# y of eight heads in one burst, the gate's samples in pairs, and three other moves in a one-layer hybrid decoder step

## The chip, the cores and the metric

The kernel runs on one core of a Trainium2 chip. The metric is the device time of one execution in microseconds. It computes in float32 throughout; its large matrix products run as three products of split operands (below). The engines are named as in the profile: PE (TensorE) with its weight loads PEld, DVE (VectorE), ACT (ScalarE), POOL (GpSimd) and SP, which issues most DMAs.

## The reference

One layer with two parts, for 256 rows of a prompt and 8 × 8 sample rows (320 columns together):

```
h    = rms_norm(x) ; proj = h @ w_in           # 2048 -> gate u, gate v, z, x|B|C, dt
gate_out = gelu(u) * (tril(W_s) @ layer_norm(gelu(v)) + b_s)     # 16 heads of 128, chunks of 128 rows
xBC  = silu(causal_conv4(xBC)) ; dt = softplus(dt + bias)
y    = (C B^T * exp(segment sums of dt*a)) @ (x*dt)              # inside a chunk, per head
     + exp(da) * C @ state                                       # from the state before the chunk
ssm_out = rms_norm_by_group((y + d*x) * silu(z))                 # 32 heads of 64 in 4 groups
state' = decay * state + B^T (decay * x * dt)
x1   = x + rms_norm([gate_out | ssm_out] @ w_out)
out  = x1 + rms_norm( (gelu(g) * u) @ w_down ),  g, u = causal_conv3(rms_norm(x1) @ w_up)
```

The gate's sample rows use the first 8 × 8 corner of W_s of each head. Outputs are the rows, the last states, the last rows of both convolutions and LayerNorm's rows of the last chunk (chunk_v).

## The kernel before

All activations stand transposed, features on the 128 partitions and the 320 rows of prompt and samples in the columns. A weight comes from HBM in slabs of 128 × 1024. ACT rounds a slab (`whi`, L128), DVE takes the remainder (`wlo`, L130), each with three buffers. For each 128 × 128 block PE runs three matmuls of 320 columns, whi·h_hi (L141), whi·h_lo (L142) and wlo·h_hi (L143). `project` does this for the columns of w_in and w_up into four large PSUM buffers (`ps`), `chunk_out` for w_out by 512 of its rows (`pd`), whose result DVE adds up in `acc`.

The work between these streams is written as generators. `project` and `chunk_out` call `tick()` at set places, which runs the next piece of the first generator up to its next `yield`. From that order of emission and from priorities, the framework that builds the program decides each engine's order by its own model of when things are ready; on the chip each engine takes its instructions strictly in that order. `tc.issue_after(x)` asks that an instruction be placed behind x.

Small results share four PSUM buffers (`misc`, tag ms): transposes, the gate's `sg`, y (`y_ps`), the sums of squares and the last states (`fin_ps`).

The pieces that the change touches:

- `layer_norm` (L651): after v of the gate is made and turned, its rows `vt` (64 of samples in the third block) are normalised in quarters of 512 columns. A quarter needs a row of the gains `lg` and one of the biases `lb` on all partitions. Each has two buffers, loaded by POOL's DMA queue. The third and fourth quarters' loads (L669) are emitted behind the steps that free a buffer.
- `gate_mix` (L689), once for each group of four heads: two matmuls of 128 columns for the prompt's chunks (L710), one of 64 columns for the samples (L711) with `wS`, the masked corner spread to 64 × 64 and zero in the lower 64 partitions. All are plain fp32.
- `ssd` (L769), once for each of four groups of eight heads, 128 × 128 pieces of fp32. `decays` makes for one head the matrix of decays times C·B from the running sums `cs` (loaded from DRAM for each pair of heads): DVE subtracts and clips in three pieces (L889), ACT takes the exponential (L891), DVE multiplies (L893). For each pair ACT also makes `cpx` (L882) and POOL multiplies it by C. `products` (L896) then runs y of a pair: eight matmuls in column halves of PE, each of which is two in the trace, and a DVE addition (L914). Today four heads' decays are followed by two pairs' products, then the other four.
- the convolution's `silu` on ACT (L426 and L427), which needs another table of ACT than the exponential.
- the stage of x1 (`x1_ready`, L1031): behind the last `pd`, DVE scales and adds x (L1036, L1037), ACT rounds (L370, `h_hi`), DVE takes the remainder (L371, `h_lo`), and the first product with w_up can start. Beside it `renewals` (L1147) adds the last states of groups 1 to 3 on POOL (L1158) and stores them by ACT's DMA queue (L1159).

Of the kernel before, what the change touches and what calls it, by code (L numbers as in the profile page):

```python
# [9 lines left out]
F32 = mybir.dt.float32  # L10
# [7 lines left out]
P = 128  # L18
NP = 256
# [15 lines left out]
def hybrid_step(  # L35
# [357 lines left out]
    with ExitStack() as mctx:  # L393
# [3 lines left out]
        pts = op.tile([P, 24, 3], F32, name="pts")  # L397
        LP = 347

        def conv_proj(c0, k0, out, soon=0):  # L400

            def evac(j, ps):
                with tc.high_priority(offset=soon) if soon else nullcontext():
                    conv(j, ps)

            def conv(j, ps):
                k = k0 + j
                pad = spare_pads.pop(0) if spare_pads and j % 2 else op.tile([P, LP], F32, tag="pad", name="pad", bufs=3)
                tokp = pad[:, 259:347].rearrange("p (b r) -> p b r", r=11)
                with first():  # L410
                    pool.memset(pad[:, 0:3], 0.0)
                    pool.tensor_copy(tokp[:, :, 0:3], sst[:, k])
# [12 lines left out]
                o = out(j)  # L425
                act.activation(o[:, :NP], t[:, :NP], AF.Silu)  # L426
                act.activation(o[:, NP:NT].rearrange("p (b t) -> p b t", b=NB),  # L427
                               t[:, 259:347].rearrange("p (b r) -> p b r", r=11)[:, :, 0:TS], AF.Silu)
            project(w_in, c0, evac, quiet=4)

        def heads_in(g):
# [117 lines left out]
        with tc.tile_pool(name="gp", bufs=1) as gp:  # L549
# [14 lines left out]
            for q in (2, 3):  # L564
                dve.tensor_tensor(out=heads4, in0=heads4, in1=ident[:, NH * q:NH * q + NH], op=ALU.add)

            wS = gp.tile([P, 4, NB, TS], F32, name="wS")
            pool.memset(wS[NS:], 0.0)

            x_asked = []  # L570
            x_sq = []
# [19 lines left out]
                            dve.tensor_tensor(out=acc[:, 0:2, :], in0=acc[:, 0:2, :], in1=acc[:, kt:kt + 2, :], op=ALU.add)  # L591

            def turned(g, vf):
                if g == 0:
                    pool.memset(vt[NS:, 2], 0.0)
                for c, (o, n) in enumerate(TOK):
                    ps = misc("vt_ps")
                    for j in range(4):
                        pe.transpose(ps[:n, P * j:P * j + P], vf[:, j, o:o + n], ident)  # L599
                    act.copy(vt[:n, c, 512 * g:512 * g + 512], ps[:n])  # L600
# [50 lines left out]
            def layer_norm():  # L651

                mv = gp.tile([P, 3, 2], F32, name="mv")
                pool.memset(mv, 1.0)
                for c, (o, n) in enumerate(TOK):
                    st = gp.tile([P, 4, 6], F32, tag="bn", name="bn", bufs=2)
                    for q in range(4):
                        dve.bn_stats(st[:n, q, :], vt[:n, c, 512 * q:512 * q + 512])
                    dve.bn_aggr(mv[:n, c, :], st[:n].rearrange("p a b -> p (a b)"))
                    yield  # L660
                lr = rsqrt_of(mv[:, :, 1], 1.0, 3)
                rows = []

                def load(q):
                    cs = slice(512 * q, 512 * q + 512)
                    for name, src in (("lg", gate_ln_g), ("lb", gate_ln_b)):
                        rows.append(gp.tile([P, 512], F32, tag=name, name=name, bufs=2))
                        with tc.issue_after(after_v[0]):
                            pool.dma_start(rows[-1], src[0:1, cs].broadcast_to([P, 512]))  # L669
                load(0)  # L670
                load(1)
                yield
                for q in range(4):
                    for c, (o, n) in enumerate(TOK):
                        v = vt[:n, c, 512 * q:512 * q + 512]
                        dve.scalar_tensor_tensor(out=v, in0=v, scalar=mv[:n, c, 0:1], in1=rows[2 * q][:n], op0=ALU.subtract, op1=ALU.mult)
                        dve.scalar_tensor_tensor(out=v, in0=v, scalar=lr[:n, c:c + 1], in1=rows[2 * q + 1][:n], op0=ALU.mult, op1=ALU.add)
# [10 lines left out]

            def gate_mix(g, uf, res):  # L689
                wT = gp.tile([P, 4, P], F32, tag="wT", name="wT", bufs=1)  # L690
                w8 = gp.tile([NS, 4, TS], F32, tag="w8", name="w8", bufs=1)
# [6 lines left out]
                with tc.issue_after(rsqrt_ins[1]):  # L698
                    dve.tensor_tensor(out=wT, in0=wT, in1=upper.unsqueeze(1).to_broadcast([P, 4, P]), op=ALU.mult)
                    for j in range(4):  # L700
                        dve.tensor_tensor(out=wS[:NS, j], in0=w8[:, j].unsqueeze(1).to_broadcast([NS, NB, TS]),
                                          in1=upper_s[:NS].rearrange("p (b t) -> p b t", b=NB), op=ALU.mult)
                yield
                hi, lo = out_parts(hp, "o")
                res += hi, lo
                for j in range(4):
                    fs = slice(512 * g + P * j, 512 * g + P * j + P)
                    ps = misc("sg")
                    for c in range(2):
                        pe.matmul(ps[:, P * c:P * c + P], vt[:, c, fs], wT[:, j, :], start=True, stop=True)  # L710
                    pe.matmul(ps[:, NP:NT], vt[:, 2, fs], wS[:, j].rearrange("p b t -> p (b t)"), start=True, stop=True)  # L711
# [32 lines left out]
        with tc.tile_pool(name="sd", bufs=1) as sd:  # L744
# [23 lines left out]

            def ssd(g):  # L769

                xs = x_of[g]
                h0 = 8 * g
                bs = slice(P * g, P * g + P)

# [6 lines left out]

                def load_sums(j):

                    cs = sd.tile([P, 2, NT], F32, tag="cs", name="cs", bufs=3)
# [50 lines left out]
                pe.matmul(ps, btok[:, 0, bs], x0d, start=True, stop=True)  # L835
# [40 lines left out]
                def decays(hl):  # L876
                    j, i = hl // 2, hl % 2
                    at = places(hl)
                    if i == 0:
                        cs = sums_of.pop(j)  # L880
                        cpx = sd.tile([P, 2, P], F32, tag="cpx", name="cpx", bufs=2)
                        act.activation(cpx, cs[:, :, at[1][0]:at[1][0] + P], AF.Exp)  # L882
# [31 lines left out]
                    dve.scalar_tensor_tensor(out=y, in0=y, scalar=d_col[:, 4 * g + j:4 * g + j + 1], in1=ps[:, :NT],  # L914
                                             op0=ALU.mult, op1=ALU.add)
# [12 lines left out]

# [126 lines left out]
    with tc.tile_pool(name="fp", bufs=1) as fp:  # L1055
# [91 lines left out]
        def renewals():  # L1147
# [7 lines left out]
            for g, s1, x1d, _ in rest:  # L1155
                yield
                yield
                pool.tensor_tensor(out=s1, in0=s1, in1=x1d, op=ALU.add)  # L1158
                act.dma_start(o_ssm_p[g], s1)  # L1159

            def load(g, i):

# [148 lines left out]
def laid_out(a):  # L1311
# [7 lines left out]
    def states(v, n):  # L1319
# [20 lines left out]
        "gate_w8": np.concatenate([w8] * NB),  # L1340
# [43 lines left out]
```

## Time and profile before

| | us |
|---|---|
| median of three runs | 1774.44 (1773.45 to 1777.11) |
| profiled execution | 1774.31 |
| its span | 1772.6 |
| mean granted TensorE clock | 0.999 |

The profile's page gives the busy time of each engine in the span, the chain of work that ended last (followed back from the last instruction through what released each step), and groups of instructions. The trace beneath it gives single instructions by time. A row of the timeline has the start, the length, the engine, the line, the operation with output and inputs, the tile of PE that it uses, shapes, how many are taken together, and in brackets the idle time before it with what ended it. On PE the length of a matmul is longer than its step to the next one, since they overlap. What a matmul costs is the difference of two starts.

### The profile page before, as it was taken

What the parts mean: (1) busy time and instruction counts of PE and PEld (TensorE: products, weight loads), DVE (VectorE), ACT (ScalarE), POOL (GpSimd) and SP (SyncE); (2) the same over time, 40 slices, a digit from 0 to 9 for tenths busy, and PEclk for the clock granted to TensorE, in tenths of its full rate; (3) what the DMA queues carried; (4) which work ended last, traced back from release to release, by engine and by line L of the source; (5) the groups of instructions that cost most, each with busy time, mean ns of one, the idle gap of its engine ahead of it and who ended that gap; (6) DMA issues with size and microseconds to landing.
All of it is one profiled execution on the core that took longest, in us unless ns stands there. A gap on an engine that the chain in (4) does not pass through costs nothing.

```text
span 1772.6 us, 31221 instructions
## 1 busy us (share of the span) xinstructions
PE 1765.2 (100%) x12223; PEld 1740.8 (98%) x12223; DVE 1183.2 (67%) x2052; ACT 800.8 (45%) x1111; POOL 281.5 (16%) x593
## 2 busy tenths in 40 slices
PE   9999999999999999999999999999999999999998
PEld 9999999999999999998999999999999999999998
DVE  7448854657877777678866666666666565656475
ACT  7344545333545454445645434343434343433335
POOL 2003210000111111012322212021101010101004
PEclk9999999999999999999999999999999999999999
DMA  7455554445664644444555656566554444444443
GB/s 251 138 167 167 191 156 149 155 152 183 226 208 150 206 154 151 154 164 155 169 190 191 210 177 201 188 196 200 185 187 153 148 155 147 157 148 152 153 148 107
DMA packets 228562, 303.04 MB, mean 171 GB/s; under 512 B 19488, under 2 KB 150656, under 8 KB 228224
## 3 DMA queue, kind: packets, MB, share of 16 engines
q1 hardware_dynamic: 216560, 281.27, 49.6%
q10 hardware_dynamic: 10448, 15.57, 2.4%
q0 software_dynamic: 1408, 4.23, 0.8%
q8 instruction: 96, 1.57, 0.4%
q14 instruction: 50, 0.41, 0.1%
HBM read 283.44 MB, written 17.58 MB: 170 GB/s over the span
## 4 chain that ended last, share of the span: by engine, by line
PE 98%; DVE 1%; DMA 0%; issue 0%; SPq 0%; POOL 0%; ACT 0%; DVEq 0%; ACTq 0%
PE ps L141 21%; PE ps L143 21%; PE ps L142 21%; PE pd L141 10%; PE pd L142 10%; PE pd L143 10%; PE y_ps L904 1%; PE sg L710 0%; PE yo_ps L853 0%; PE up_ps L1198 0%; PE tsum L282 0%; PE xt_ps L382 0%; PE vt_ps L599 0%; DMA vf<-in_w_in 0%; PE s_ps L835 0%; PE x1p L1233 0%
## 5 line engine op out<-in xcount | busy, mean ns | idle before, releaser
L130 DVE TENSOR_TENSOR wlo<-wraw,whi 128x1024 fp32r<-128x1024 f32 x470 | 581.4, 1237 | 383.2 <-ACT whi L128 380.6
L128 ACT CAST whi<-wraw 128x1024 fp32r<-128x1024 f32 x470 | 492.2, 1048 | 703.0 <-PE ps L142 411.5
L141 PE MATMUL ps<-h_hi,whi 128*128 128x320 f32 x2528 | 782.7, 310 | 0.0
L142 PE MATMUL ps<-h_lo,whi 128*128 128x320 f32 x2528 | 780.2, 309 | 1.4 <-DVE h_lo L371 1.4
L143 PE MATMUL ps<-h_hi,wlo 128*128 128x320 f32 x2528 | 779.7, 309 | 0.2 <-DVE wlo L130 0.2
L142 PEld LDWEIGHTS ps<-h_lo,whi 128*128 128x128 f32 x2528 | 475.0, 188 | 2.8 <-DVE h_lo L371 1.9
L141 PEld LDWEIGHTS ps<-h_hi,whi 128*128 128x128 f32 x2528 | 474.7, 188 | 3.1 <-issue 1.6
L143 PEld LDWEIGHTS ps<-h_hi,wlo 128*128 128x128 f32 x2528 | 474.6, 188 | 0.9 <-DVE wlo L130 0.7
L141 PE MATMUL pd<-fhi,whi 128*128 128x320 f32 x704 | 217.3, 309 | 0.0
L143 PE MATMUL pd<-fhi,wlo 128*128 128x320 f32 x704 | 217.3, 309 | 0.0
L142 PE MATMUL pd<-flo,whi 128*128 128x320 f32 x704 | 217.3, 309 | 0.0
L141 PE MATMUL pd<-ohi,whi 128*128 128x320 f32 x448 | 138.7, 310 | 0.0
L142 PE MATMUL pd<-olo,whi 128*128 128x320 f32 x448 | 138.6, 310 | 0.0
L143 PE MATMUL pd<-ohi,wlo 128*128 128x320 f32 x448 | 138.3, 309 | 0.0
L142 PEld LDWEIGHTS pd<-flo,whi 128*128 128x128 f32 x704 | 132.1, 188 | 0.7
L143 PEld LDWEIGHTS pd<-fhi,wlo 128*128 128x128 f32 x704 | 132.1, 188 | 0.0
L141 PEld LDWEIGHTS pd<-fhi,whi 128*128 128x128 f32 x704 | 132.1, 188 | 0.0
L234 DVE TENSOR_TENSOR acc_ffn<-acc_ffn,pd 128x320 f32<-128x320 f32 x160 | 77.3, 483 | 33.2 <-PE pd L143 32.0
L1091 POOL COPY ptf<-pad 128x2 f32<-128x2 f32 x88 | 22.6, 258 | 405.6 <-DVE pad L1079 405.0
L141 PEld LDWEIGHTS pd<-ohi,whi 128*128 128x128 f32 x448 | 84.1, 188 | 0.9 <-issue 0.4
L142 PEld LDWEIGHTS pd<-olo,whi 128*128 128x128 f32 x448 | 84.1, 188 | 0.7 <-issue 0.4
L143 PEld LDWEIGHTS pd<-ohi,wlo 128*128 128x128 f32 x448 | 84.1, 188 | 0.2 <-issue 0.2
(303 smaller groups left out, 1582.6 us busy)
## 6 DMA issues: line engine op xcount, KB each, us to landing
wraw<-in_ffn_w_up SPq DMA_DIRECT2D x176, 512.0 KB, 3.5
wraw<-in_w_in SPq DMA_DIRECT2D x142, 512.0 KB, 3.5
wraw<-in_ffn_w_down SPq DMA_DIRECT2D x88, 512.0 KB, 3.3
wraw<-in_w_out SPq DMA_DIRECT2D x64, 512.0 KB, 3.3
st<-in_state_ssm SPq DMA_DIRECT2D x64, 256.0 KB, 4.6
out_ssm_state_sample<-st ACTq DMA_DIRECT2D x32, 256.0 KB, 2.6
cs<-dacs_d SPq DMA_DIRECT2D x16, 320.0 KB, 4.5
xr<-in_xT SPq DMA_DIRECT2D x4, 640.0 KB, 4.6
```

Of the source, the lines that this page charges most:

```text
L128: act.copy(hi[:, :m], raw[:, :m])
L130: dve.tensor_tensor(out=lo[:, :m], in0=raw[:, :m], in1=hi[:, :m].bitcast(F32), op=ALU.subtract)
L141: pe.matmul(ps, whi, xhi, start=first, stop=False)
L142: pe.matmul(ps, whi, xlo, start=False, stop=False)
L143: newest[0] = pe.matmul(ps, wlo, xhi, start=False, stop=last).ins
L234: dve.tensor_tensor(out=acc[:, nb, :], in0=acc[:, nb, :], in1=ps[:, :NT], op=ALU.add)
L904: pe.matmul(ps[64 * i:64 * i + 64, cols], w(hl), x(hl, m, cpx), tile_position=(0, 64 * i), **flags)
L1091: pool.tensor_copy(ptf[:, k, :], pad[:, 256:258])
```

## The change

1. `ssd`: all eight heads' decays come first, then four pairs' products in one go. `cs` and `cpx` get four buffers, and all four loads of cs are asked for together.
2. `gate_mix`: the sample rows of an odd head are copied by DMA (POOL's queue, behind LayerNorm's quarters) into the lower 64 partitions of the even head's columns, and `wS` becomes block diagonal for two heads, so that one matmul of 128 columns serves both. The odd head has none.
3. `renewals`: additions and stores of the last states are put under `issue_after(whole[KD - 1])`, the last split of x1.
4. `layer_norm`: all eight row loads are emitted ahead of the quarters; those of the last two go into two buffers of the tag vf.
5. `ssd`: the exponential of cpx comes under `issue_after(last_silu)`.

The scratch for DMAs that POOL issues goes from 4096 to 1024.

```diff
+                made = act.activation(o[:, NP:NT]..., AF.Silu)
+                silus.append(made.ins)
...
-            wS = gp.tile([P, 4, NB, TS], F32, name="wS")
-            pool.memset(wS[NS:], 0.0)
+            wS = gp.tile([P, 2, 2, NB, TS], F32, name="wS")
+            pool.memset(wS, 0.0)
...
-                if g == 0:
-                    pool.memset(vt[NS:, 2], 0.0)
...
-                load(0)
-                load(1)
+                both = [("lg", gate_ln_g), ("lb", gate_ln_b)]
+                for q in range(2):
+                    rows.append([load(q, src, gp.tile([P, 512], F32, tag=name, name=name, bufs=2)) for name, src in both])
+                late = [gp.tile([P, 4, NT], F32, tag="vf", name=name, bufs=2).rearrange("p k n -> p (k n)") for name, _ in both]
+                for q in range(2):
+                    rows.append([load(2 + q, src, row[:, 512 * q:512 * q + 512]) for row, (_, src) in zip(late, both)])
...
-                        if c == 2 and q < 2:
-                            load(q + 2)
+                        if c == 2:
+                            two = vt[:, 2, 512 * q:512 * q + 512].rearrange("p (i r f) -> p i r f", r=2, f=P)
+                            pool.dma_start(two[NS:, :, 0], two[:NS, :, 1])
...
-                    pe.matmul(ps[:, NP:NT], vt[:, 2, fs], wS[:, j].rearrange("p b t -> p (b t)"), start=True, stop=True)
+                    if j % 2 == 0:
+                        pe.matmul(ps[:, NP:NP + 2 * NS], vt[:, 2, fs], wS[:, j // 2].rearrange("p r b t -> p (r b t)"), start=True, stop=True)
+                        of_two = ps[:, NP:NP + 2 * NS].rearrange("p (r b t) -> p r b t", r=2, b=NB)
...
-                                      in0=ps[:, NP:NT].rearrange("p (b t) -> p b t", b=NB),
+                                      in0=of_two[:, j % 2],
...
-                xs = x_of[g]
+                xs, last_silu = x_of[g], silus[-1]
...
-                sums_of = {j: load_sums(j) for j in range(3)}
+                sums_of = {j: load_sums(j) for j in range(4)}
...
-                        act.activation(cpx, cs[:, :, at[1][0]:at[1][0] + P], AF.Exp)
+                        with tc.issue_after(last_silu):
+                            act.activation(cpx, cs[:, :, at[1][0]:at[1][0] + P], AF.Exp)
...
-                for j in range(0, 4, 2):
-                    for hl in range(2 * j, 2 * j + 4):
-                        decays(hl)
-                        yield
+                for hl in range(8):
+                    decays(hl)
                     yield
+                yield
+                for j in range(4):
                     products(j)
-                    products(j + 1)
-                    if j == 0:
-                        sums_of[3] = load_sums(3)
...
-                pool.tensor_tensor(out=s1, in0=s1, in1=x1d, op=ALU.add)
-                act.dma_start(o_ssm_p[g], s1)
+                with tc.issue_after(whole[KD - 1]):
+                    pool.tensor_tensor(out=s1, in0=s1, in1=x1d, op=ALU.add)
+                    act.dma_start(o_ssm_p[g], s1)
...
-    nc = _bacc.Bacc("TRN2", target_bir_lowering=False, num_devices=1, dynamic_dma_scratch_size=4096)
+    nc = _bacc.Bacc("TRN2", target_bir_lowering=False, num_devices=1, dynamic_dma_scratch_size=1024)
```

What this makes of the engines' orders is shown at three places. First PE at group 1's last y, before (y_ps is y of a pair of heads, xt_ps the transposes of the next group's x, pd the product with w_out):

```order
L141 MATMUL pd_11_6327<-ohi,whi 128x320
L904 MATMUL y_ps<-cs,xdt 64x128
L382 MATMUL xt_ps<-ident,xs 128x128 x2
L904 MATMUL y_ps<-cs,xdt 64x128 x3
L904 MATMUL y_ps<-cpx,s_5500 64x128 x2
L904 MATMUL y_ps<-cs,xdt 64x64 x2
L382 MATMUL xt_ps<-ident,xs 128x128 x6
```

and now, at the only y of group 1 (the rows between are three more pairs of the same form):

```order
L143 MATMUL pd_5_6123<-ohi,wlo 128x320
L912 MATMUL y_ps<-cs,xdt 64x128 x4
L912 MATMUL y_ps<-cpx,s_5465 64x128 x2
L912 MATMUL y_ps<-cs,xdt 64x64 x2
...
L142 MATMUL pd_6_6208<-olo,whi 128x320
L382 MATMUL xt_ps<-ident,xs 128x128 x3
L143 MATMUL pd_6_6208<-ohi,wlo 128x320
```

Y of group 1 was spread over six pieces with 95, 21 and fewer stream matmuls between; now all 32 matmuls stand together, 120 stream matmuls behind yo, with five of them before the first transposes. In groups 0 and 2 two bursts 72 matmuls apart become one at 120 behind yo, in group 3 (59 and 72) one at 118.

Second PE at one group of the gate, before and now (sg is the gate's sum of a head, vt LayerNorm's rows):

```order
L710 MATMUL sg<-wT,vt 128x128 x2
L711 MATMUL sg<-wS,vt 128x64
```

```order
L715 MATMUL sg<-wT,vt 128x128 x2
L717 MATMUL sg<-wS,vt 128x128
L715 MATMUL sg<-wT,vt 128x128 x4
L717 MATMUL sg<-wS,vt 128x128
L715 MATMUL sg<-wT,vt 128x128 x2
```

The first piece stood four times in a group, once for each head: twelve matmuls. Now there are ten, and the sample matmul has 128 columns.

Third POOL and ACT in the stage of x1. POOL with its waits, before and now (sq is a sum of squares, s a group's state, pad the up-projection's rows):

```order
L300 TENSOR_TENSOR sq_8507<-sq_8507,sq 128x320 [waits Activation_49,Pool_49] x11
L1158 TENSOR_TENSOR s_5500<-s_5500,x1d 128x512 [waits Activation_49]
L1076 MEMSET pad 128x2 [waits DMAHW3_49,DMAHW4_49,DMAHW2_49,DMAHW5_49,DMAHW1_49,DMAHW6_49,DMAHW0_49,DMAHW7_49,DVE_49,PE_49]
```

```order
L300 TENSOR_TENSOR sq_8500<-sq_8500,sq 128x320 [waits Activation_49,Pool_49] x11
L1164 TENSOR_TENSOR s_5465<-s_5465,x1d 128x512 [waits Activation_49]
L1081 MEMSET pad 128x2 [waits DMAHW3_49,DMAHW4_49,DMAHW2_49,DMAHW5_49,DMAHW1_49,DMAHW6_49,DMAHW0_49,DMAHW7_49,DVE_49,PE_49]
```

The addition stands three times in a row in both, at the same place, and waits for the same engine at the same count. ACT there, before and now (h_hi the rounded x1, x1d the copy of fin_ps):

```order
L1014 COPY x1d<-fin_ps 128x512
L1159 DMA out_ssm_state_prompt<-s_5500 128x512
L370 ACTIVATE h_hi<-acc_mix,prm 128x320
L1041 COPY x1d<-fin_ps 128x512
L370 ACTIVATE h_hi<-acc_mix,prm 128x320
```

```order
L370 ACTIVATE h_hi<-acc_mix,prm 128x320 x4
L1165 DMA out_ssm_state_prompt<-s_5465 128x512
L128 CAST whi<-wraw 128x1024
L1165 DMA out_ssm_state_prompt<-s_6378 128x512
L1165 DMA out_ssm_state_prompt<-s_7382 128x512
L128 CAST whi<-wraw 128x1024
```

On ACT the three stores moved from among the first copies to behind the last ones.

More of the change, by code (lines that the diff above doesn't have):

```diff
@@ L398, in hybrid_step @@
         LP = 347
+        silus = []
         def conv_proj(c0, k0, out, soon=0):
@@ L426, in conv @@
                 act.activation(o[:, :NP], t[:, :NP], AF.Silu)
-                act.activation(o[:, NP:NT].rearrange("p (b t) -> p b t", b=NB),
-                               t[:, 259:347].rearrange("p (b r) -> p b r", r=11)[:, :, 0:TS], AF.Silu)
+                made = act.activation(o[:, NP:NT].rearrange("p (b t) -> p b t", b=NB),
+                                      t[:, 259:347].rearrange("p (b r) -> p b r", r=11)[:, :, 0:TS], AF.Silu)
+                silus.append(made.ins)
             project(w_in, c0, evac, quiet=4)
@@ L662, in layer_norm, with load @@
                 rows = []
[L664 to L669, printed above, removed]
-                load(0)
-                load(1)
+                def load(q, src, row):
+                    with tc.issue_after(after_v[0]):
+                        pool.dma_start(row, src[0:1, 512 * q:512 * q + 512].broadcast_to([P, 512]))
+                    return row
+                both = [("lg", gate_ln_g), ("lb", gate_ln_b)]
[4 more added lines that the diff above has]
+                    rows.append([load(2 + q, src, row[:, 512 * q:512 * q + 512]) for row, (_, src) in zip(late, both)])
                 yield
@@ L675, in layer_norm @@
                         v = vt[:n, c, 512 * q:512 * q + 512]
-                        dve.scalar_tensor_tensor(out=v, in0=v, scalar=mv[:n, c, 0:1], in1=rows[2 * q][:n], op0=ALU.subtract, op1=ALU.mult)
-                        dve.scalar_tensor_tensor(out=v, in0=v, scalar=lr[:n, c:c + 1], in1=rows[2 * q + 1][:n], op0=ALU.mult, op1=ALU.add)
-                        if c == 2 and q < 2:
-                            load(q + 2)
+                        dve.scalar_tensor_tensor(out=v, in0=v, scalar=mv[:n, c, 0:1], in1=rows[q][0][:n], op0=ALU.subtract, op1=ALU.mult)
+                        dve.scalar_tensor_tensor(out=v, in0=v, scalar=lr[:n, c:c + 1], in1=rows[q][1][:n], op0=ALU.mult, op1=ALU.add)
+                        if c == 2:
+                            two = vt[:, 2, 512 * q:512 * q + 512].rearrange("p (i r f) -> p i r f", r=2, f=P)
+                            pool.dma_start(two[NS:, :, 0], two[:NS, :, 1])
                         yield
@@ L700, in gate_mix @@
                     for j in range(4):
-                        dve.tensor_tensor(out=wS[:NS, j], in0=w8[:, j].unsqueeze(1).to_broadcast([NS, NB, TS]),
-                                          in1=upper_s[:NS].rearrange("p (b t) -> p b t", b=NB), op=ALU.mult)
+                        rs = slice(NS * (j % 2), NS * (j % 2) + NS)
+                        dve.tensor_tensor(out=wS[rs, j // 2, j % 2], in0=w8[rs, j].unsqueeze(1).to_broadcast([NS, NB, TS]),
+                                          in1=upper_s[rs].rearrange("p (b t) -> p b t", b=NB), op=ALU.mult)
                 yield
@@ L782, in load_sums @@
                 def load_sums(j):
-                    cs = sd.tile([P, 2, NT], F32, tag="cs", name="cs", bufs=3)
+                    cs = sd.tile([P, 2, NT], F32, tag="cs", name="cs", bufs=4)
                     o = NS * (j // 2)
@@ L880, in decays @@
                         cs = sums_of.pop(j)
-                        cpx = sd.tile([P, 2, P], F32, tag="cpx", name="cpx", bufs=2)
-                        act.activation(cpx, cs[:, :, at[1][0]:at[1][0] + P], AF.Exp)
+                        cpx = sd.tile([P, 2, P], F32, tag="cpx", name="cpx", bufs=4)
+                        with tc.issue_after(last_silu):
+                            act.activation(cpx, cs[:, :, at[1][0]:at[1][0] + P], AF.Exp)
                         pool.tensor_tensor(out=cpx, in0=cpx, in1=cT[:, g, P:2 * P].unsqueeze(1).to_broadcast([P, 2, P]),
@@ L1339, in laid_out @@
         "gate_wT": w_s.transpose(2, 0, 1),
-        "gate_w8": np.concatenate([w8] * NB),
+        "gate_w8": np.concatenate([w8] * (P // TS)),
         "gate_b_s": a["gate_b_s"], "ssm_dt_bias": a["ssm_dt_bias"], "ssm_a_log": a["ssm_a_log"],
```

2 lines of the change are left out of this document (1 added, 1 removed).

## The prediction

> **What bounds the kernel now.** I read the page first, then the chain of waits, then what PE waits for, then the timelines of the five places that the change touches.
>
> ```profile
> PE 1765.2 (100%) x12223; PEld 1740.8 (98%) x12223; DVE 1183.2 (67%) x2052; ACT 800.8 (45%) x1111; POOL 281.5 (16%) x593
> PE 98%; DVE 1%; DMA 0%; issue 0%; SPq 0%; POOL 0%; ACT 0%; DVEq 0%; ACTq 0%
> L128 ACT CAST whi<-wraw 128x1024 fp32r<-128x1024 f32 x470 | 492.2, 1048 | 703.0 <-PE ps L142 411.5
> PE ps L142 <- DVE h_lo L371: 1.4, 2, 1.2
> PE s_ps L835 <- POOL xde L821: 0.2, 1, 0.2
> ```
>
> PE is busy for 1765.2 of 1772.6 us and carries 98% of the chain. The work that feeds it has room: ACT's weight split L128 stood idle 411.5 us because it waited for PE. So time can only come from fewer or shorter PE instructions, from fewer joints between different kinds of them, or from the few places where something holds PE up. Of those the list of PE's waits (the last two rows, from that view) has one over a microsecond, 1.4 us on h_lo in the x1 stage. A microsecond off DVE, ACT or POOL is worth nothing elsewhere. The step of the steady stream, from the timeline:
>
> ```profile
> 181.79 0.31 PE L143 MATMUL ps<-h_hi,wlo 128*128 128x320 f32 x1
> ...
> 187.07 0.31 PE L143 MATMUL ps<-h_hi,wlo 128*128 128x320 f32 x1
> ```
>
> 36 matmuls in 5.28 us: 0.147 us each, start to start (the 0.31 is latency).
>
> **y of eight heads in one burst.** PE's timeline at group 0's first y of four heads:
>
> ```profile
> 477.94 0.31 PE L143 MATMUL pd<-ohi,wlo 128*128 128x320 f32 x1
> 478.18 0.66 PE L904 MATMUL y_ps<-cs,xdt 128*64 128x128 f32 x8
> 478.67 0.39 PE L904 MATMUL y_ps<-cpx,s 128*64 128x128 f32 x4
> 478.89 0.72 PE L904 MATMUL y_ps<-cs,xdt 128*64 128x64 f32 x12
> 479.44 0.39 PE L904 MATMUL y_ps<-cpx,s 128*64 128x128 f32 x4
> 479.66 0.28 PE L904 MATMUL y_ps<-cs,xdt 128*64 128x64 f32 x4
> 479.87 0.42 PE L141 MATMUL pd<-ohi,whi 128*128 128x320 f32 x1
> 480.13 0.31 PE L142 MATMUL pd<-olo,whi 128*128 128x320 f32 x1
> ```
>
> Two heads repeat after 479.44 − 478.67 = 0.77 us. The burst lasts 479.87 − 478.18 = 1.69, which is 2 × 0.77 and 0.15 for its start. The change of kind costs more at both ends: 478.18 − 477.94 = 0.24 before it and 480.13 − 479.87 = 0.26 after it, against 0.147, so 0.09 and 0.11. A burst thus has a fixed price of 0.15 + 0.20 = 0.35 us. The matmuls themselves stay the same in number and shape. In groups 0, 2 and 3 two bursts become one (the chain lists 1.69 twice in each): 3 × 0.35 = **1.05 us**. Group 1 is scattered now, and the chain shows six pieces:
>
> ```profile
> 490.70 1.69 PE y_ps L904 x32
> ...
> 559.27 0.36 PE y_ps L904 x2
> ...
> 560.41 1.69 PE y_ps L904 x27
> ...
> 576.22 0.36 PE y_ps L904 x2
> ...
> 577.08 0.91 PE y_ps L904 x13
> ...
> 581.27 0.36 PE y_ps L904 x2
> ...
> 582.00 0.92 PE y_ps L904 x13
> ```
>
> They sum to 4.60 us; one burst of eight heads takes 0.15 + 4 × 0.77 = 3.23: 1.37 less. Five pairs of joints go as well, at most 5 × 0.20 = 1.0; the last two pieces stand beside transposes, whose own joints with the stream remain or even get one more place, so I take 0.75. Group 1 gives **2.1 us** (1.4 to 2.4).
>
> **Gate's samples in pairs.** One head of the gate on PE's timeline:
>
> ```profile
> 259.97 0.66 PE L710 MATMUL sg<-wT,vt 128*128 128x128 f32 x4
> 260.47 0.33 PE L711 MATMUL sg<-wS,vt 128*128 128x64 f32 x2
> 260.64 0.66 PE L710 MATMUL sg<-wT,vt 128*128 128x128 f32 x4
> ```
>
> A head takes 260.64 − 259.97 = 0.67 us for six passes (each fp32 matmul runs as two), 0.112 a pass, although two of the six move 64 columns and the others 128. So the step is not set by the columns, and a sample pass of 128 columns should cost the same 0.112. Now two heads share one sample matmul: 24 passes of a group become 20. 4 × 0.112 = 0.45 in each of four groups: **1.8 us**. Bounds: nothing more than this, and 1.4 if the wide passes bring back 0.02 each at the joints. The price is paid outside PE: four copies of 64 rows of vt by POOL's DMA queue behind LayerNorm. Each cost POOL about the 0.54 of a load's issue in the row at 172.01 below and a landing of some 4 us, and nobody reads them before 259.36, over 70 us later. wS's clearing on POOL and its products on DVE are as many as before. Nothing on PE.
>
> **LayerNorm's rows early.** POOL's and DVE's timelines, two pieces of the chain on PE:
>
> ```profile
> 172.01 0.54 POOL L669 DMA_DIRECT2D lb<-in_gate_ln_b  x1 [0.40 <-DVE vt L677]
> ...
> 175.53 0.75 DVE L677 SCALAR_TENSOR_TENSOR vt<-vt,rs_r,lb 128x512 f32<-128x512 f32 x1 [3.81 <-DMA lb<-in_gate_ln_b]
> ...
> 181.29 0.37 PE ps L143
> ...
> 187.38 0.27 PE ps L141
> ```
>
> The third and fourth quarter's lb is issued only when DVE has freed a row, and DVE then stands 3.81 us before it. Its weight splits fall behind, and 6 and 12 us later two of PE's steps last 0.37 and 0.27 in place of 0.147: 0.22 + 0.12 = **0.35 us**. Now all eight loads go ahead of the LayerNorm in POOL's order, the late ones into buffers of vf that are free some 35 us earlier, so DVE does not stand. If the two steps had another cause, 0.
>
> **Last states' additions.** The timeline of the x1 stage (POOL, DVE, PE):
>
> ```profile
> 814.35 1.26 POOL L1158 TENSOR_TENSOR s<-s,x1d 128x512 f32<-128x512 f32 x1 [7.11 <-ACT x1d L1014]
> ...
> 814.91 1.05 DVE L1037 TENSOR_TENSOR acc_mix<-acc_mix,xr 128x320 f32<-128x320 f32 x1
> ...
> 816.80 0.48 DVE L1037 TENSOR_TENSOR acc_mix<-acc_mix,xr 128x320 f32<-128x320 f32 x1
> ...
> 817.14 2.76 POOL L1158 TENSOR_TENSOR s<-s,x1d 128x512 f32<-128x512 f32 x2 [1.53 <-ACT x1d L1041]
> 817.20 1.55 DVE L371 SCALAR_TENSOR_TENSOR h_lo<-acc_mix,prm,h_hi 128x320 fp32r<-128x320 f32 x1
> ...
> 818.81 0.41 PE L142 MATMUL ps<-h_lo,whi 128*128 128x320 f32 x1 [1.17 <-DVE h_lo L371]
> ...
> 820.30 0.41 PE L142 MATMUL ps<-h_lo,whi 128*128 128x320 f32 x1 [0.20 <-DVE h_lo L371]
> ```
>
> DVE's addition of xr takes 1.05 us beside POOL's first addition and 0.48 when POOL is quiet, and the 1.55 of h_lo falls under POOL's other two. This is what holds PE for 1.17 and 0.20. Freed of it PE would win 1.4 from the waits and up to 0.57 (1.05 − 0.48) at the head of the stage, 1.9 together. But I count **nothing**. The new wait names the last h_hi copy, an ACT instruction, and the order of instructions shows what it reaches: ACT's three output DMAs move behind the last x1 copies, while POOL's three additions keep their place and wait for ACT's copy of fin_ps as before. The ACT issues that move wait for nothing that PE needs. Bounds: −1.9 if the additions do move, and +0.3 if the moved issues delay a weight split.
>
> The Trainium skill, page "SBUF — State Buffer", on the shared port pair, says that a DVE instruction with two SBUF inputs and a GpSimd instruction that reads SBUF exclude each other, the second one standing until the first is done. The row agrees: POOL's first addition ends at 814.35 + 1.26 = 815.61, and DVE's ends 0.35 later. By the rule the term is 1.9 if the additions are moved and nothing if only their DMAs are, as by the rows.
>
> **Exponentials behind the last silu.** The lists of instructions have 31 loads of ACT's tables before and 23 after, and a row for one is:
>
> ```profile
> 479.20 1.28 ACT L882 ACT_TABLE_LOAD   x1
> 577.93 1.22 DVE L130 TENSOR_TENSOR wlo<-wraw,whi 128x1024 fp32r<-128x1024 f32 x1
> 582.95 0.55 DVE L914 SCALAR_TENSOR_TENSOR xs<-xs,prm,y_ps 128x320 f32<-128x320 f32 x1 [0.24 <-PE y_ps L904]
> ```
>
> That is 8 × 1.28 = 10.2 us off ACT, which is idle over half the span: nothing on the time. What it adds is a wait: everything behind a cpx exponential on ACT stands until the last silu. The other exponentials and weight splits are queued there, and the splits' slack (411.5 us in all) covers them.
>
> **The wait that the burst may bring.** The four y of a group use the four small PSUM buffers at once. In group 1 five matmuls (0.73 us) later transposes need one back, and that takes DVE's addition L914 (0.55, rows just above), which may stand behind a weight split (1.22). At best the first addition is done while PE still runs the other heads: 0. At worst a split and all four additions stand behind the burst: 1.22 + 4 × 0.55 − 0.73 = 2.7. Since the first y is complete 2.4 us before the last, I am near the lower end: **+0.5**, one addition late.
>
> **The sum:** −1.05 − 2.1 − 1.8 − 0.35 + 0 + 0.5 = −4.8. The profiled execution took 1774.31 us (its span 1772.6 and 1.7 around it), 0.13 under the median of the runs, 1774.44; from it: **1769.5 us**. With the terms' own bounds alone: 1.05 + 2.4 + 1.8 + 0.35 = 5.6 gives 1768.7, and 1.05 + 1.4 + 1.4 − 2.7 = 1.15 gives 1773.2.
>
> **Rivals.** *The additions really move.* Then x1 gives its 1.9 too: 1767.6 us. For it speaks the contention in the rows, against it POOL's unchanged order and waits. 5%.
>
> *The gain is half eaten.* New waits at the transposes behind group 1's and group 2's burst, 1.3 to 3.7 us over my own sum, or joints that do not pay: 1771.5 (1770.8 to 1773.2). For it speaks DVE, with 1.22 us splits between everything, and that a burst of 3.4 us asks for four additions in a row; against it that PE has hardly any wait on DVE in the trace (1.4 + 0.2). 21%.
>
> *The other side: the burst waits for the last head.* Until now four heads' decays had to be there for the first half, and the other four had 12 us more. If DVE's products of heads 6 and 7 come one split and one product late (1.22 + 0.48) in each of four groups, PE stands 4 × 1.7 = 6.8 us: with the other terms, −5.3 + 6.8 = +1.5, 1775.8. It decides from 1.3 us a group. For it speaks that the burst now stands some 120 matmuls behind yo, where the second half stood at 144 in groups 0 and 2, so 24 × 0.147 = 3.5 us earlier; and that DVE has eight operations for each pair of heads to put among its splits. Against it: 120 matmuls are 17.6 us, cs is asked for at once for all four pairs, and ACT switches no tables between them. 8%, with a tail to 1779.
>
> My own forecast keeps 66%, with a range of 1768.5 to 1770.8.
>
> **Chances.** A measurement of this kernel can tell about 0.2%, 3.5 us: faster by that means under 1770.9. Forecast and first rival lie there (71%), of which I take off some for the runs' own spread (1773.45 to 1777.11): faster 0.67, within 0.2% 0.26, slower 0.07. The range reaches to the first rival below and through most of the second above: 1767.0 to 1772.8.
>
> **What would show it.** Right: y in one piece of 3.2 us in each group's chain; the gate's group 2.15 us in place of 2.6; no wait of DVE for lb; PE's steps at 181 and 187 at 0.147; at x1 PE still waiting 1 to 1.4 us for h_lo with POOL's additions at the same place. Wrong: sample passes over 0.112; a row of PE waits with xt_ps or y_ps behind DVE over 1 us; h_lo at x1 under 0.6 us, which would mean that the additions moved; or a stall in a place that the change does not touch.

## The result and the profile after

| | before | changed |
|---|---|---|
| median of 18 runs | 1774.58 us | 1771.57 us |
| lowest to highest | 1773.27 to 1777.11 | 1770.64 to 1772.92 |
| profiled execution, span | 1772.6 | 1771.0 |

The ratio is 0.9983 (95% interval 0.9977 to 0.9990): 3.0 us faster, 0.17%. The forecast was 4.8 us; the measured time lies outside the 1768.5 to 1770.8 that the forecast kept for itself, where the rival "the gain is half eaten" was put. Engine totals and the shares of the chain, from the page of the changed kernel:

```profile
PE 1760.5 (99%) x12207; PEld 1737.3 (98%) x12207; DVE 1185.5 (67%) x2052; ACT 789.5 (45%) x1103; POOL 267.9 (15%) x596
...
PE 93%; DVE 3%; DMA 1%; issue 1%; ACT 1%; SPq 0%; POOL 0%; DVEq 0%; ACTq 0%; POOLq 0%
```

PE has 4.7 us less work, but DVE, transfers and ACT now hold 5% of the chain where they held 1%. PE's own gain came as reckoned; a part of it was given back as waiting. One group of the gate and group 0's y on PE's timeline (to be read by differences of starts):

```profile
260.32 0.60 PE L715 MATMUL sg<-wT,vt 128*128 128x128 f32 x4
260.76 0.39 PE L717 MATMUL sg<-wS,vt 128*128 128x128 f32 x2
260.98 1.06 PE L715 MATMUL sg<-wT,vt 128*128 128x128 f32 x8
261.88 0.39 PE L717 MATMUL sg<-wS,vt 128*128 128x128 f32 x2
262.10 0.61 PE L715 MATMUL sg<-wT,vt 128*128 128x128 f32 x4
262.47 0.39 PE L141 MATMUL ps<-h_hi,whi 128*128 128x320 f32 x1
...
486.13 0.66 PE L912 MATMUL y_ps<-cs,xdt 128*64 128x128 f32 x8
...
489.36 1.12 PE L938 MATMUL fin_ps<-x1d,btok 128*128 128x512 f32 x2
```

The gate's group takes 262.47 − 260.32 = 2.15 us, where it took 2.59. A sample pass with 128 columns costs (260.98 − 260.76)/2 = 0.11, as one with 64. The burst of eight heads takes 489.36 − 486.13 = 3.23.

Where the rest went is seen on DVE just ahead of group 0's state (the bracket is the idle time before a row and what ended it), first before, then changed:

```profile
445.71 2.07 DVE L889 TENSOR_SCALAR cs<-cs,nda 128x128 f32<-128x128 f32 x7 [1.78 <-DMA cs<-dacs_d]
447.71 1.21 DVE L130 TENSOR_TENSOR wlo<-wraw,whi 128x1024 fp32r<-128x1024 f32 x1
448.84 1.90 DVE L889 TENSOR_SCALAR cs<-cs,nda 128x64 f32<-128x64 f32 x7
450.66 1.22 DVE L130 TENSOR_TENSOR wlo<-wraw,whi 128x1024 fp32r<-128x1024 f32 x1
451.79 0.47 DVE L889 TENSOR_SCALAR cs<-cs,nda 128x128 f32<-128x128 f32 x2
453.91 1.23 DVE L130 TENSOR_TENSOR wlo<-wraw,whi 128x1024 fp32r<-128x1024 f32 x1 [1.65 <-ACT whi L128]
```

```profile
445.44 2.05 DVE L897 TENSOR_SCALAR cs<-cs,nda 128x128 f32<-128x128 f32 x8 [2.32 <-DMA cs<-dacs_d]
447.41 1.21 DVE L130 TENSOR_TENSOR wlo<-wraw,whi 128x1024 fp32r<-128x1024 f32 x1
448.54 3.45 DVE L897 TENSOR_SCALAR cs<-cs,nda 128x128 f32<-128x128 f32 x10
451.91 1.21 DVE L130 TENSOR_TENSOR wlo<-wraw,whi 128x1024 fp32r<-128x1024 f32 x1
453.04 1.25 DVE L897 TENSOR_SCALAR cs<-cs,nda 128x128 f32<-128x128 f32 x6
455.15 1.22 DVE L130 TENSOR_TENSOR wlo<-wraw,whi 128x1024 fp32r<-128x1024 f32 x1 [0.86 <-ACT whi L128]
```

With buffers and transfers for all four pairs, DVE makes 24 subtractions here in place of 16, and it stands 2.32 us for the transfer. The third split comes at 455.15 in place of 453.91, although the changed kernel reached this stretch 0.87 us earlier. PE's 168 stream matmuls between the transposes and s_ps take 26.51 us there, and 24.73 before: 1.8 us of the gain are gone. About 0.5 us more goes in the stream behind group 0's y, and 0.45 at group 1's transposes, whose chain is:

```profile
571.48 1.02 DVE cv L423
...
572.52 0.43 ACT xs L428
...
572.99 0.77 PE xt_ps L382 x5
```

One more difference is not the change's. A transfer of x that is asked for at 4.09 us took 5.75 us in this execution and 4.46 in the one of before (3.8 to 4.9 in the eleven runs below), and the chain of the changed kernel runs through it. PE's 201st stream matmul starts at 38.3 us here, at 37.0 before, and between 36.7 and 37.4 in the eleven runs. So the profiled span understates the gain (1.6 us against 3.0 in the medians) by these 1.3 us.

### The profile page after: what moved, and what is told of

Same layout as the page of the kernel before. It is cut to its first block, busy times and chain, and to the rows that moved or that the text cites. A ratio compares the mean times of both kernels' runs of the same rounds, so it can differ in the third digit from the quotient of the medians.

```text
span 1771.0 us, 31185 instructions
## 1 busy us (share of the span) xinstructions
PE 1760.5 (99%) x12207; PEld 1737.3 (98%) x12207; DVE 1185.5 (67%) x2052; ACT 789.5 (45%) x1103; POOL 267.9 (15%) x596
## 4 chain that ended last, share of the span: by engine, by line
PE 93%; DVE 3%; DMA 1%; issue 1%; ACT 1%; SPq 0%; POOL 0%; DVEq 0%; ACTq 0%; POOLq 0%
PE ps L141 20%; PE ps L143 20%; PE ps L142 20%; PE pd L141 10%; PE pd L143 10%; PE pd L142 10%; DVE wlo L130 1%; DMA cs<-dacs_d 1%; PE y_ps L912 1%; PE yo_ps L860 0%; PE up_ps L1204 0%; PE sg L715 0%; PE tsum L282 0%; DVE cs L897 0%; DMA wraw<-in_ffn_w_up 0%
```

## The experiments

Times are medians; "to before" is the difference to the median of before taken in the same session (1774.6 for the changed kernel; 1774.4, 1774.3 and 1774.2 in the three sessions of the experiments). PE's excess is the time of a run of stream matmuls over 0.147 us each. A profile is of one execution, which can lie over a microsecond off its run's median.

| run | median | to before | ratio, 95% interval |
|---|---|---|---|
| changed kernel | 1771.57 | −3.0 | 0.9977 to 0.9990 |
| burst alone | 1776.83 | +2.4 | 1.0002 to 1.0019 |
| all but the burst | 1772.62 | −1.8 | 0.9982 to 1.0000 |
| gate's pairs alone | 1773.37 | −1.1 | 0.9984 to 1.0002 |
| rows early alone | 1773.77 | −0.4 | 0.9988 to 1.0005 |
| changed, no guard on the exponentials | 1774.40 | +0.1 | 0.9994 to 1.0012 |
| changed, additions behind x1 | 1776.18 | +1.8 | 0.9999 to 1.0016 |
| the same, stored by POOL's queue | 1772.66 | −1.6 | 0.9984 to 1.0001 |
| changed, additions later, POOL's queue | 1770.41 | −3.9 | 0.9973 to 0.9991 |
| changed, half of the decays late | 1769.62 | −4.7 | 0.9967 to 0.9984 |
| both repairs | 1767.89 | −6.3 | 0.9951 to 0.9976 |
| both, all decays of groups 0 and 1 late | 1767.50 | −6.7 | 0.9946 to 0.9974 |

**The burst alone.** The kernel before with this edit (and the smaller scratch):

```diff
-                sums_of = {j: load_sums(j) for j in range(3)}
+                sums_of = {j: load_sums(j) for j in range(4)}
...
-                        cpx = sd.tile([P, 2, P], F32, tag="cpx", name="cpx", bufs=2)
+                        cpx = sd.tile([P, 2, P], F32, tag="cpx", name="cpx", bufs=4)
...
-                for j in range(0, 4, 2):
-                    for hl in range(2 * j, 2 * j + 4):
-                        decays(hl)
-                        yield
+                for hl in range(8):
+                    decays(hl)
                     yield
+                yield
+                for j in range(4):
                     products(j)
-                    products(j + 1)
-                    if j == 0:
-                        sums_of[3] = load_sums(3)
...
```

> Only the burst of eight heads (with its buffers of cs and cpx) on the kernel before. Theory (late splits): PE's own part of the burst gives 3.1 us, but DVE makes the decays of all eight heads of group 0 before 455 us, the weight splits behind them come late and PE gives back 1.8 there and about 0.5 at group 1's transposes: net 0.8, about 1773.8 us, with PE's stream between the transposes and s_ps of group 0 some 1.8 us over 168 x 0.147. Rival (another part of the change costs the 2 us): the burst alone gives its whole 3.1, 1771.5 us, and that stretch shows no excess.

1776.83 us, slower than either kernel. Both expectations were wrong in the sum, though the late splits are there (1.76 us of excess in the 168 matmuls). The chain at group 1 shows a cost that neither had:

```profile
570.13 4.53 DMA cs<-dacs_d
...
575.02 1.28 ACT L882
576.32 0.42 ACT cpx L882
576.75 1.10 ACT L426
578.05 0.42 ACT xs L426
578.52 0.44 PE xt_ps L382 x2
```

The burst frees cs, new cs is fetched, and ACT takes an exponential of cpx that waits for that transfer. Behind it stand another load of ACT's tables, the last silu of the next group, and PE's transposes. PE loses 2.1 us in twelve matmuls there, and another 0.7 in one step behind group 2's y.

**All but the burst.** The changed kernel with the old two halves, three buffers of cs and two of cpx.

> The changed kernel without the burst: y again in two halves, the other four parts kept. Theory (late splits): gate 1.8 + rows 0.35 remain, nothing else: 1774.6 - 2.15 = 1772.4 us, no excess of PE between 438 and 465 us. Rival (another part costs 2 us): that part is still in, 1774.4 us.

1772.62 us, and the 168 matmuls have their old length. So no other part holds the missing 1.8 us, and the burst with its guard is worth the difference of −3.0 to −1.8, some 1.2 us of its 3.1.

**The gate's pairs alone, and the rows alone.** Parts 2 and 4 of the change on the kernel before.

> Only the gate's samples in pairs on the kernel before. Theory: four passes fewer in each group, 4 x 0.45 = 1.8 us: 1772.8 us, the group 2.2 us long on PE in place of 2.6. Rival (the copies of the sample rows on POOL's queue hold up LayerNorm or splits and give some back): 1773.5 us or more, with new idle time on DVE between 168 and 190 us.

> Only LayerNorm's rows early on the kernel before. Theory: DVE's wait for lb goes, and PE's steps near 181 and 187 us are 0.147: 0.35 to 0.8 us less, 1774.0 us. Rival (the later loads on POOL's queue collide with something else): no gain, 1774.5 us.

Neither is told from no change by time alone. On PE the gate's four groups take 8.6 us in place of 10.4, 1.8 less as forecast. The run of the pairs alone lacks the early rows, and there DVE still waits 3.5 us for lb; the 480 matmuls behind the turning of the gate's v (those behind 135 us) have 0.90 us of excess, before 0.42, with the burst alone 0.79. With the rows early, alone or in the changed kernel, it is 0.07. Of the burst's 0.79, some 0.5 is a step at 159 us, ahead of the wait for lb at 176, and not its doing. So this wait costs about 0.25 to 0.8 us, from execution to execution.

**The guard on the exponentials.** The changed kernel without it:

```diff
-                        with tc.issue_after(last_silu):
-                            act.activation(cpx, cs[:, :, at[1][0]:at[1][0] + P], AF.Exp)
+                        act.activation(cpx, cs[:, :, at[1][0]:at[1][0] + P], AF.Exp)
```

> The changed kernel without its fifth part: the exponentials of cpx no longer behind the last silu. Theory (the guard pays for the burst): with eight heads' decays at once ACT takes an exponential of cpx, which waits for its transfer of cs, ahead of the last silu of the next group; silu, and PE's transposes behind it, come 2 us late in group 1, as in the run of the burst alone: about 1774 us, and a wait of PE over 1.5 us near 575 us. Rival (the guard is worth nothing, the burst alone lost its time by the other placement of its tiles): 1771.6 us as the changed kernel.

1774.40 us: about 3 us by this one line (0.1 over before in place of 3.0 under it). The trace has nearly all of it where the theory put it: with as many matmuls between, PE takes 79.09 us from the state of group 1 to that of group 2 in place of the changed kernel's 77.27, and 89.11 from there to group 3's in place of 88.16. What PE waited for in that run, the first row:

```profile
PE xt_ps L382 <- ACT xs L428: 1.6, 1, 1.6
```

**Half of the decays late.** In groups 0 and 1, for heads 4 to 7:

```diff
-                        with tc.issue_after(last_silu):
+                        with tc.issue_after(s1_there if g < 2 and hl >= 4 else last_silu):
                             act.activation(cpx, cs[:, :, at[1][0]:at[1][0] + P], AF.Exp)
...
+                        with tc.issue_after(cb_there) if g < 2 and hl >= 4 else nullcontext():
                             dve.tensor_scalar(out=m[:, o:o + n], in0=m[:, o:o + n], scalar1=nda[:, c, h0 + hl:h0 + hl + 1],
...
```

Here `s1_there` is the copy of the first state and `cb_there` C·B's mask.

> The changed kernel, in which in groups 0 and 1 the decays of heads 4 to 7 (DVE's subtractions and the cpx exponentials) stand behind C.B's mask on DVE and the copy of the first state on ACT, and no longer ahead of the weight splits at 445 to 455 us. Theory (late splits): PE's excess between 438 and 465 us falls from 1.8 to under 0.3 and that after group 0's y from 0.9 to 0.5: 1.8 us less, 1769.8 us, unless the burst now waits. Rival (the splits are late because the transfers of cs, which compete with slabs, hold DVE up, whatever the number of heads): the excess stays over 1 us, 1771.6 us.

1769.62 us, 1.7 us better than the changed kernel when each is taken to its own session's before. PE's waits for splits in this stretch fell to one step of 0.85 us, so the theory has its time but not its "under 0.3": the rival has a share. DVE now waits 3.59 us for cs at 445 us with only the first four heads to do, and 3.01 us behind group 0's y, which costs PE a step of 1.15 us at 495:

```profile
491.23 0.29 DVE L898 TENSOR_SCALAR cs<-cs,nda 128x128 f32<-128x128 f32 x1 [3.01 <-DMA cs<-dacs_d]
```

So this execution, which lies 1.0 us over its run's median, gives back behind y what it won ahead of the state: from the first of the 168 matmuls to group 1's state PE takes 71.8 us in it, as in the changed kernel. With the same edit in the run of both repairs below it takes 69.9.

The other profiled executions tell the two causes apart. This is DVE's wait for cs at 443 to 446 us beside what PE loses in the 168 matmuls against before:

| profiled execution | DVE's wait for cs | PE's loss |
|---|---|---|
| eight heads early: stored by POOL's queue | 1.28 | 0.8 |
| burst alone | 1.86 | 1.7 |
| additions later | 1.89 | 1.4 |
| changed kernel | 2.32 | 1.8 |
| no guard | 2.88 | 2.4 |
| additions behind x1 | 3.12 | 2.6 |
| four heads early: both repairs | 2.34 | 0.0 |
| half of the decays late | 3.59 | 0.8 |

With eight heads the loss grows with the wait, if not from each row to the next, and at the same wait of 2.3 us it is 1.8 us smaller with four heads ahead of the splits than with eight. So the heads and the transfer add up, and how late the transfer lands changes from execution to execution.

**Additions really behind x1's split.** A one-column copy on POOL reads the last h_lo, and the additions go behind it:

```diff
+            there = tp.tile([P, 1], F32, tag="there", name="x1_there", bufs=1)
+            gate = pool.tensor_copy(there, hT[1][:, KD - 1, 0:1].bitcast(F32)).ins
...
-                with tc.issue_after(whole[KD - 1]):
+                with tc.issue_after(gate):
                     pool.tensor_tensor(out=s1, in0=s1, in1=x1d, op=ALU.add)
+                with tc.issue_after(whole[KD - 1]):
                     act.dma_start(o_ssm_p[g], s1)
```

> The changed kernel, in which POOL's three additions of the last states really stand behind the last split of x1 (a one-column copy on POOL of the last h_lo comes first, and the additions behind it). Theory (POOL and DVE hold each other up): h_lo falls from 1.5 to 0.54 us, the first addition of x from 0.93 to 0.48, PE's wait for h_lo from 1.4 to about 0.2: 1.7 us less than the changed kernel, 1769.9 us. Rival (the wait comes from DVE's own order of work, and POOL's share in it is small): less than 0.5 us, about 1771.4 us, with h_lo still over 1 us.

At x1 the theory holds: h_lo falls to 0.55 us and PE's wait for it to 0.2. Yet the run is 1776.18 us, far over both expectations. Two rows of its ACT:

```profile
845.38 3.79 ACTq L1168 DMA_DIRECT2D out_ssm_state_prompt<-s  x3
849.35 1.05 ACT L128 CAST whi<-wraw 128x1024 fp32r<-128x1024 f32 x1 [8.87 <-POOL s L1166]
```

ACT, whose order is fixed, reached the first store and stood for POOL's addition with a weight split behind it; it did no work for 8.87 us. Then the sum of squares came late, by the list of PE's waits:

```profile
PE tsum L282 <- DVE sq L300: 2.3, 1, 2.3
```

**Stores by POOL's queue; additions later.** The first run only replaces the store by `pool.dma_start`. In the second, the additions moreover stand behind the last copy on POOL of the first up-projection, about 873 us.

> As the run with POOL's additions behind x1's split, but the three states are stored by POOL's own queue and not by ACT's. Theory (ACT's queue stood): in that run the gain at x1 was made and lost again because ACT, which issues the stores, stood 8.9 us for POOL with weight splits behind it; without this about 1.5 us under the changed kernel, 1770.1 us, and no wait of PE over 0.5 us between 840 and 865 us. Rival (POOL's additions collide with DVE's sum of squares there): PE still waits 1 us or more at 845 to 863 us, and the time is 1772 us or more.

> The changed kernel with the additions still later, behind the first up-projection's last copy on POOL (about 870 us), and stored by POOL's queue. Theory (the collision is with work that PE waits for, and there is none there): 1.5 to 1.9 us under the changed kernel, 1769.9 us, with h_lo at 0.55 us and no new wait of PE. Rival (the additions collide with the convolution's work on DVE): PE waits at 865 to 900 us, and 1771 us or more.

The first gives 1772.66: by the medians the stores on ACT had cost 3.4 us of the 4.8 by which the run lay over the changed kernel. The traces show 2.1 of the 3.4 in place: from x1's first `spread` matmul (the one that lays the rows' scale on all partitions) to the next sum of squares on PE (`tsum`) it is 47.7 us in the changed kernel, 49.3 with the stores on ACT and 47.2 with POOL's queue. Where the other 1.3 lie stays open; the profiled execution with the stores on ACT was 1.7 us under its median. The rest was the rival: PE waits 1.8 us for the sum of squares in that run, and DVE's square additions stand beside POOL's:

```profile
842.36 2.13 DVE L300 TENSOR_TENSOR sq<-sq,sq 128x320 f32<-128x320 f32 x2
...
842.85 1.29 POOL L1166 TENSOR_TENSOR s<-s,x1d 128x512 f32<-128x512 f32 x1
```

Two square additions take 2.13 us there, 1.02 in the changed kernel at the same place. The second run moves POOL past them: 1770.41 us, 0.9 under the changed kernel. It has no PE wait for h_lo or the sum of squares. The later place is nearly free: one step of PE lasts 0.34 us at 902 (0.49 at 899 in the run of both repairs, none in the run with all decays late), shortly behind the third addition; whether by it was not tried. The gain is less than the 1.5 expected, and what ate the rest was not tried either. Its profile shows two differences that are no part of the edit: 1.1 us more behind group 0's y than in the changed kernel's, and a granted clock of 0.5 for 3.4 us from 811.3, in which two matmuls of `fin_ps` start 0.85 us apart in place of 0.43. From `spread` to the sum of squares it takes 46.2 us, and 45.2 in the run with all decays late, which has the additions at the same place and the full clock there. The same drop lies in this stage in the execution of before (from 812.2) and not in the changed kernel's.

**Both repairs, and all decays late.** The first joins half of the decays late with the additions later. In the second the condition on heads 4 to 7 is dropped.

> The changed kernel with both repairs: heads 4 to 7 of groups 0 and 1 late (2.0 us measured alone) and the additions behind the first up-projection's copies, stored by POOL's queue (1.2 measured alone). Theory (two stages, nothing in common): 1771.6 - 3.2 = 1768.4 us. Rival (they meet in some later wait): 1769.5 us, the better of the two.

> As the run with both repairs, and now all eight heads' decays of groups 0 and 1 stand behind C.B's mask and the first state's copy. Theory (DVE stands for the transfers of cs with splits queued behind): DVE's waits for cs at 445 and 488 us (3.6 and 3.0 us in the run of the half late) go, and PE's steps of 0.85 and 1.15 us at 448 and 495 us with them, another 1.2 us: 1767.2 us. Rival (the burst of group 0 then waits for its last head, 120 matmuls being 17.6 us for 24 subtractions and 8 products among splits): PE waits for cs ahead of y_ps of group 0, and the time is 1768.5 us or more.

1767.89 and 1767.50 us: the repairs add up (the medians of each alone sum to 5.5 us under before, and 6.3 are measured in five runs), and the second beats both kernels of this case, 6.7 us under the one before. Its gain over the first is within the spread of five runs, so its own theory is not settled by time. All that PE still waits for in it:

```profile
PE early L70 <- DVE ones L66: 1.1, 1, 1.1
PE ps L141 <- ACT whi L128: 0.4, 1, 0.4
PE spread L290 <- DVE rs_r L268: 0.2, 1, 0.2
PE x1p L1278 <- DVE acc_ffn L1268: 0.2, 1, 0.2
PE xt_ps L382 <- ACT xs L428: 0.2, 1, 0.2
PE ps L142 <- DVE h_lo L371: 0.2, 1, 0.2
```

The burst of group 0 takes 3.47 us there in place of 3.23, so it lost at most 0.24 us to its last head and not the stall of the rival. DVE's waits for cs are 3.1 us in all, 6.9 in the changed kernel, and PE's loss in the 168 matmuls is gone.

## Why the prediction was right, and where not

The sum was 4.8 us and the gain 3.0. The time lies inside the range because that was drawn through the second rival, and this is partly luck: the rival named late additions at the transposes behind the bursts, and of that only 0.45 us came, by another cause. What ate the gain stood elsewhere.

**Gate, 1.8 us:** right in mechanism and size, 1.77 us on PE. **Rows, 0.35:** right, 0.36 in the two profiles, with a spread of about 0.25 to 0.8 in others.

**The burst on PE, 3.15 us:** right. The y bursts went from 14.75 to 12.94 us, 1.81, where the steps of the sum had 0.45 in groups 0, 2 and 3 and 1.37 in group 1. The joints in the stream gave about 1.1 and group 1's transposes 0.4, where 1.35 were forecast.

**Last states, 0:** right, and for the reason given. Two rows of the changed kernel beside those shown of before:

```profile
814.84 2.80 POOL L1164 TENSOR_TENSOR s<-s,x1d 128x512 f32<-128x512 f32 x2 [1.49 <-ACT x1d L1046]
814.93 1.56 DVE L371 SCALAR_TENSOR_TENSOR h_lo<-acc_mix,prm,h_hi 128x320 fp32r<-128x320 f32 x1
```

POOL's additions kept their place, and h_lo stands under them as before. What the rule of the Trainium skill (page "SBUF — State Buffer", the shared port pair) says of two such instructions agrees with the run in which they are apart: 0.55 us in place of 1.56. The bound of 1.9 us holds for the stage (from the first `spread` matmul to PE's fourth matmul with h_lo it is 6.42 us in the changed kernel, 4.60 with the additions moved), but it was too simple all the same: an addition that is moved lands on other work, and behind x1's split that is the sum of squares, on which PE waits.

**The wait at group 1's transposes, +0.5:** the size is right (0.45), the cause is not. PE waited for the last silu, which came late because DVE's convolution did (chain above), and not for a PSUM buffer behind y's addition.

**"Behind the last silu", nothing on the time:** wrong, though the sum did not show it, since it left out both the cost and what takes it away. The guard was priced as tables saved on an engine with slack, and the splits' slack of 411 us was taken as cover. But slack over the span says nothing of an engine's order at one place. Without the guard an exponential that waits for a transfer stands ahead of the silu that PE waits for: about 3 us, shown by the run without it. In the sum this is no gain: the guard buys back what the burst costs, so parts 1 and 5 are one part.

**The step that failed, left out of the sum: the early decays.** The sum had no term for DVE's work being pulled forward. The buffers of the burst allowed 24 subtractions, with waits for transfers, ahead of weight splits in group 0: 1.8 us in the profiled execution. That this is just the difference between 4.8 and 3.0 is chance: with eight heads early the loss there is 0.8 to 2.6 us from execution to execution, and some 0.5 more goes behind group 0's y. The rival of the burst that waits for its last head looked for lateness at the burst; what came was work too early, in front of something urgent. By the medians the half-late run takes 1.7 us back, and the run with all decays late has no loss in that stretch.

## What to carry to other kernels

More buffers for an off-path engine let its order pull work forward, also work that waits for a transfer; look at what is queued behind that wait. When a change merges a burst, ask for both ends: what its inputs now stand in front of, and what the buffers it frees set going. Check in the engines' orders what a guard moves: here the one that named an instruction of ACT moved ACT's stores and left POOL's additions where they were. And a store that waits for another engine belongs on a queue with nothing urgent behind it.

## What was not expected of the hardware

Transfers of cs (320 KB) took 8.5 us at 437 us in the changed kernel, beside states and slabs, with the DMA engines 90% busy or more in most slices from 434 to 448 us; in the same stretch before they took 7.9, where the page of the kernel before has 4.5 as the median of all. The first of them took 7.4 us in one execution with eight heads early and 9.3 in another, and PE's loss went with it. One transfer at the start took 5.75 us in one execution and 4.46 in another, and in some executions the granted clock falls to 0.5 for 3.4 us in the stage of x1. Each is worth up to 1 or 2 us, as much as a part of this change, so traces are compared here by stage and not by span.
